# Scores of the first token tile as three float32r products in a two-layer decoder trunk

## The chip, the cores and the metric

The kernel runs on one core of a Trainium2 chip. The metric is the device time of one execution in microseconds (us), lower is better. Engines are called PE (TensorE, matrix products), DVE (VectorE), ACT (ScalarE), POOL (GpSimd) and SP (the DMA queue used for the weights).

## What is computed

Two decoder layers on 256 tokens of width 2048, in float32. The first layer normalises, projects to queries, keys, values and gates, and runs two attention mixers: A with 16 query heads on 2 key heads and a window of 128, B with 16 heads and a mixture of dilated windows. The second layer is a spatial gating unit and has no attention. What the change touches is the score of a query with the keys that it may see:

```python
nb = -(-L // BLK)
qb = _blocks(q, nb)
kb = _with_prev(_blocks(k, nb))
vb = _with_prev(_blocks(v, nb))
s = jnp.einsum('bgrnqd,bgnkd->bgrnqk', qb, kb) + bias[:, :, None]
s = jnp.where(_band_mask(nb, max_dist), s, NEG)
```

With blocks of 128 and 256 tokens there are two query tiles. The second sees the keys of both tiles (256), the first only its own (128).

## The kernel before, in words

**Split products.** A weight product in float32 is written as three products of float32r operands (`gemm`, L121 to L123): a high half times a high half, high times low and low times high. The high half is a cast by ACT (`whi`, L85), the low half the rest, taken by DVE (`wlo`, L86). A weight tile comes by SP's queue, is split once, four tiles ahead at most, and used in twelve products of 512 columns.

**Fillers.** Everything of attention is put between the weight products. `gemm` calls `fill()` after every second group of three products, which advances the first generator in the list `fillers` by one step. So the generators `attn_a` (twice) and `attn_b` (twice) yield after pieces of work: first transpositions of keys and queries, then `attention`. After this a scheduler settles the order on each engine from the program's order and its own estimate of times. So small shifts can appear in the order away from the lines that are edited.

**Queries and keys.** `pair_T` (L218) transposes two 128-column pieces of both token tiles into the one PSUM bank with the tag `t`: four PE instructions. `q_T` reads this bank three times: ACT writes the high half of the second tile's queries (L230), DVE the low half (L231), ACT a float32 copy of the first tile's queries, `q0` (L234). `k_T` reads it three times too: `kh` of both tiles by ACT (L246), `kl` by DVE (L247), and a float32 copy of the first tile's keys, `k0`, by ACT (L248). The next transpositions wait until the last of the three has read. In the trace the operands `q0`, `q1` are called `q`, and `k0` is `k`.

**Scores.** `scores` works on two heads, one on rows 0 to 63 of the arrays and one on rows 64 to 127, each into a bank of its own (tag `s`, two banks). The second tile's scores, 256 columns, are the three products of L298; the first tile's, 128 columns, one float32 product, L301. DVE then adds bias and mask and takes the maximum (L307, L311), ACT takes exponentials (L321, L323). `ptrans` transposes the probabilities through bank `t` (L331, copy `pt` L333), `pv` multiplies with the values (L345 to L347, 64 columns). There are four score blocks of two heads in each of four runs of `attention`, 16 in all.

Of the kernel before, what the change touches and what calls it, by code (L numbers as in the profile page):

```python
# [10 lines left out]
F32 = mybir.dt.float32  # L11
F32R = mybir.dt.float32r
# [5 lines left out]
P = 128  # L18
# [15 lines left out]
def trunk(ctx, tc, x, xT, ev_g, w_in0, w_kva, qk_g, sinks, w_out0, od_g, w_in1, v_g, w_sT, b_s,  # L34
# [10 lines left out]
    def c4(shape, name, dt=F32):  # L45
        return big.tile(shape, dt, tag="c4", name=name)
# [174 lines left out]

    def q_T(z, scale, box):

        q0 = c4([P, 4, P], nm("q0"))
        q1 = c4([P, 2, 4, P], nm("q1"), F32R)
        box.extend((q0, q1))
        for p0 in range(0, 4, 2):
            tp = pair_T(z, p0, 2)
            ps_ = slice(p0, p0 + 2)
            nc.scalar.activation(q1[:, 0, ps_, :], tp[:, :, P:2 * P], AF.Copy, scale=scale)  # L230
            nc.vector.scalar_tensor_tensor(q1[:, 1, ps_, :], tp[:, :, P:2 * P], scale,  # L231
                                           q1[:, 0, ps_, :].bitcast(F32),
                                           op0=ALU.mult, op1=ALU.subtract)
            nc.scalar.activation(q0[:, ps_, :], tp[:, :, 0:P], AF.Copy, scale=scale)  # L234
            yield

    def k_T(z, npair, box):

        k0 = c4([P, npair, P], nm("k0"))
        kh = c4([P, npair, S], nm("kh"), F32R)  # L240
        kl = c4([P, npair, S], nm("kl"), F32R)
        box.extend((k0, kh, kl))
        for p0 in range(0, npair, 2):
            tp = pair_T(z, p0, 2)
            ps_ = slice(p0, p0 + 2)
            nc.scalar.copy(kh[:, ps_, :], tp)  # L246
            nc.vector.tensor_tensor(kl[:, ps_, :], tp, kh[:, ps_, :].bitcast(F32), op=ALU.subtract)  # L247
            nc.scalar.copy(k0[:, ps_, :], tp[:, :, 0:P])  # L248
            yield

    def qk_norm(z):
# [22 lines left out]

    def attention(mix, h0, first_bias, qTb, kTb, vfn, ydst):

        (q0, q1), (k0, kh, kl) = qTb, kTb
        bts = [first_bias, None]
        st = {}
        grp = {}  # L280
# [1 line left out]
        def scores(i0):  # L282


            if i0 % 4 == 0:
                nmx = tiny.tile([P, 4, 2], F32, tag="nmx", name=nm("nmx"))
                mx = tiny.tile([P, 4, 2], F32, tag="mx", name=nm("mx"))
                l = tiny.tile([P, 4, 2], F32, tag="l", name=nm("l"))
                grp[i0 // 4] = (bts[i0 // 4], mx, nmx, l)
            bt, mx, nmx, l = grp[i0 // 4]  # L290
            pq = i0 // 2
            kp = (h0 + i0) // 8 if mix == 0 else pq
            sps = [psum("s", 2), psum("s", 2)]
            halves = [slice(0, 64), slice(64, 128)]
            for qpart, kpart, st_, en_ in ((0, kh, True, False), (0, kl, False, False),
                                           (1, kh, False, True)):
                for sp, half in zip(sps, halves):
                    nc.tensor.matmul(sp[:, 0:256], q1[half, qpart, pq, :], kpart[half, kp, :],  # L298
                                     start=st_, stop=en_)
            for sp, half in zip(sps, halves):  # L300
                nc.tensor.matmul(sp[:, 256:384], q0[half, pq, :], k0[half, kp, :],  # L301
                                 start=True, stop=True)
            for i, sp in zip((i0, i0 + 1), sps):
                h = h0 + i
                j = i % 4
                sb = m2([P, 384], nm("sb"))
                nc.vector.tensor_tensor_reduce(out=sb[:, 0:256], in0=sp[:, 0:256],  # L307
                                               in1=bt[:, j, :],
                                               scale=1.0, scalar=NEG, op0=ALU.add, op1=ALU.max,
                                               accum_out=mx[:, j, 1:2])  # L310
                nc.vector.tensor_tensor_reduce(out=sb[:, 256:384], in0=sp[:, 256:384],  # L311
                                               in1=bt[:, j, P:2 * P],
                                               scale=1.0, scalar=NEG, op0=ALU.add, op1=ALU.max,
                                               accum_out=mx[:, j, 0:1])
                if mix == 0:
                    nc.vector.tensor_scalar(nmx[:, j, :], mx[:, j, :], snk[:, h:h + 1], -1.0,
                                            op0=ALU.max, op1=ALU.mult)
                else:
                    nc.vector.tensor_scalar(nmx[:, j, :], mx[:, j, :], -1.0, None, op0=ALU.mult)  # L319
                pr = m2([P, 384], nm("pr"))  # L320
                nc.scalar.activation(pr[:, 0:256], sb[:, 0:256], AF.Exp, bias=nmx[:, j, 1:2],  # L321
                                     accum_out=l[:, j, 1:2])
                nc.scalar.activation(pr[:, 256:384], sb[:, 256:384], AF.Exp,  # L323
                                     bias=nmx[:, j, 0:1], accum_out=l[:, j, 0:1])
                st[i] = pr
# [371 lines left out]
```

## Time and profile before

| | |
|---|---|
| median of 3 runs | 1159.23 us (1159.16 to 1159.51) |
| the profiled execution | 1158.9 us, its span 1157.1 us |
| PE | busy 1149.3 us, 99% of the span, 5498 instructions |
| DVE | busy 641.3 us, 55% |
| ACT | busy 592.7 us, 51% |
| POOL | busy 115.5 us, 10% |
| granted clock of PE | 1.0 over the span |

The span runs from the first to the last instruction. A busy PE is not a PE at its peak: products overlap, so what one costs is read from the distance between starts, not from its duration. Attention's share of the span lies between about 91 us (first key transpositions) and 354 us (last transpositions of its result).

### The profile page before, as it was taken

How to read it: one execution, taken by the hardware profiler on the slowest of the kernel's cores; microseconds unless marked ns; L12 is line 12 of the kernel's file. 1: busy time of each engine (PE TensorE's matmuls, PEld its weight loads, DVE VectorE, ACT ScalarE, POOL GpSimd, SP SyncE). 2: the span in 40 equal slices, each digit the busy share in tenths (PEclk: the TensorE clock that was granted, in tenths of full speed). 3: DMA queues.
4: the chain of work that ended last, by engine and by line, in shares of the span. 5: the costliest groups of instructions: out<-in, count | busy, mean ns of one | idle time of the engine just before them, and what ended most of it. 6: DMA issues, size and time to landing. Idle time of an engine off the chain costs nothing.

```text
span 1157.1 us, 14468 instructions
## 1 busy us (share of the span) xinstructions
PE 1149.3 (99%) x5498; PEld 952.8 (82%) x5498; DVE 641.3 (55%) x823; ACT 592.7 (51%) x820; POOL 115.5 (10%) x69
## 2 busy tenths in 40 slices
PE   9999999999999999999999999999999999999998
PEld 7887787788788888888888888888888888888887
DVE  6586567556546565544546555555555555445443
ACT  6556664644654455445445445554554455333432
POOL 0132112113012000111110000000000000000000
PEclk9999999999999999999999999999999999999999
DMA  9676435546447555666666555555556555666661
GB/s 352 224 248 208 130 117 184 172 137 226 144 143 228 185 183 182 215 204 200 213 203 193 184 181 187 177 184 194 185 168 197 182 184 172 203 207 210 197 210 38
DMA packets 63638, 218.37 MB, mean 189 GB/s; under 512 B 7632, under 2 KB 10320, under 8 KB 63312
## 3 DMA queue, kind: packets, MB, share of 16 engines
q1 hardware_dynamic: 60352, 209.74, 56.2%
q0 software_dynamic: 2080, 7.34, 2.1%
q8 instruction: 43, 0.70, 0.2%
q10 hardware_dynamic: 1136, 0.36, 0.1%
q14 instruction: 27, 0.22, 0.1%
HBM read 215.32 MB, written 2.10 MB: 188 GB/s over the span
## 4 chain that ended last, share of the span: by engine, by line
PE 95%; DVE 1%; ACT 1%; DMA 1%; issue 1%; SPq 0%; ACTq 0%
PE g L121 30%; PE g L122 30%; PE g L123 30%; PE t L331 1%; DMA wraw<-in_w_in_dram 1%; ACT whi L85 1%; DVE wlo L86 1%; PE s L298 1%; PE u L347 1%; PE u L346 1%; PE t L385 1%; PE u L345 0%; PE t L218 0%; PE s L599 0%; PE s L600 0%
## 5 line engine op out<-in xcount | busy, mean ns | idle before, releaser
L86 DVE TENSOR_TENSOR wlo<-wraw,whi 128x1024 fp32r<-128x1024 f32 (+1 forms) x393 | 512.7, 1309 | 448.8 <-ACT whi L85 447.7
L85 ACT CAST whi<-wraw 128x1024 fp32r<-128x1024 f32 (+1 forms) x393 | 408.3, 1041 | 490.8 <-PE g L123 468.0
L121 PE MATMUL g<-whi,hTh 128*128 128x512 f32 (+1 forms) x1184 | 464.2, 392 | 0.0
L122 PE MATMUL g<-wlo,hTh 128*128 128x512 f32 (+1 forms) x1184 | 459.5, 388 | 0.6 <-DVE wlo L86 0.6
L123 PE MATMUL g<-whi,hTl 128*128 128x512 f32 (+1 forms) x1184 | 458.9, 388 | 0.0
L123 PEld LDWEIGHTS g<-whi,hTl 128*128 128x128 f32 x1184 | 222.6, 188 | 45.0
L121 PEld LDWEIGHTS g<-whi,hTh 128*128 128x128 f32 x1184 | 222.8, 188 | 44.6
L122 PEld LDWEIGHTS g<-wlo,hTh 128*128 128x128 f32 x1184 | 222.8, 188 | 44.0 <-DVE wlo L86 1.4
L121 PE MATMUL g<-whi,yTh 128*128 128x512 f32 (+1 forms) x416 | 156.2, 376 | 0.0
L122 PE MATMUL g<-wlo,yTh 128*128 128x512 f32 (+1 forms) x416 | 155.3, 373 | 0.0
L123 PE MATMUL g<-whi,yTl 128*128 128x512 f32 (+1 forms) x416 | 155.3, 373 | 0.0
L123 PEld LDWEIGHTS g<-whi,yTl 128*128 128x128 f32 x416 | 78.3, 188 | 14.1
L121 PEld LDWEIGHTS g<-whi,yTh 128*128 128x128 f32 x416 | 78.4, 188 | 13.6
L122 PEld LDWEIGHTS g<-wlo,yTh 128*128 128x128 f32 x416 | 78.4, 189 | 13.5
L608 POOL TENSOR_TENSOR y<-y,gt 128x1024 f32<-128x1024 f32 x8 | 19.2, 2404 | 344.9 <-ACT gt L191 344.9
L577 POOL TENSOR_TENSOR v<-v,gv 128x1024 f32<-128x1024 f32 x8 | 22.1, 2757 | 219.5 <-ACT junk L574 219.5
L191 ACT ACT_TABLE_LOAD x20 | 25.7, 1283 | 1.7 <-PE g L123 1.4
L272 POOL TENSOR_TENSOR bias<-bias,ba 128x1024 f32<-128x1024 f32 x8 | 21.9, 2738 | 31.1 <-DMA bias<-in_bias_dram 27.8
L321 ACT ACTIVATE pr<-sb,nmx 128x256 f32<-128x256 f32 x32 | 16.2, 506 | 9.9 <-DVE nmx L319 6.6
L333 ACT COPY pt<-t 128x384 f32<-128x384 f32 x32 | 15.0, 469 | 9.8 <-PE t L331 9.8
L307 DVE CUSTOM_DVE_ANT_0 sb<-s,bias 128x256 f32<-128x256 f32 x32 | 13.3, 414 | 9.1 <-PE s L301 8.1
L588 DVE SCALAR_TENSOR_TENSOR vl<-v,rstdv,vh 128x512 fp32r<-128x512 f32 x16 | 11.3, 749 | 12.4 <-ACT vh L587 12.4
(127 smaller groups left out, 555.2 us busy)
## 6 DMA issues: line engine op xcount, KB each, us to landing
wraw<-in_w_in_dram SPq DMA_DIRECT2D x287, 512.0 KB, 3.7
wraw<-in_w_out_dram SPq DMA_DIRECT2D x96, 512.0 KB, 4.0
bias<-in_bias_dram POOLq DMA_DIRECT2D x8, 512.0 KB, 3.8
xT<-in_xT_dram SPq DMA_DIRECT2D x8, 256.0 KB, 5.0
xr<-in_x_dram SPq DMA_DIRECT2D x2, 1024.0 KB, 11.1
wraw<-in_w_kva_dram SPq DMA_DIRECT2D x8, 256.0 KB, 3.4
gv<-in_v_g_dram POOLq DMA_DIRECT2D x8, 256.0 KB, 3.1
out_dram<-o SPq DMA_DIRECT2D x7, 256.0 KB, 5.1
```

What stands on the lines that cost most here:

```text
L85: nc.scalar.copy(hi[:, js, :cw], raw[:, js, :cw])
L86: nc.vector.tensor_tensor(lo[:, js, :cw], raw[:, js, :cw], hi[:, js, :cw].bitcast(F32), op=ALU.subtract)
L121: nc.tensor.matmul(o, ah[:, sl], whi[:, k, a:b], start=st, stop=False)
L122: nc.tensor.matmul(o, ah[:, sl], wlo[:, k, a:b], start=False, stop=False)
L123: nc.tensor.matmul(o, al[:, sl], whi[:, k, a:b], start=False, stop=en)
L191: nc.scalar.activation(z[:, tt, :cw], acc[tt][:, :cw], func, scale=rs[:, tt:tt + 1])
L272: nc.gpsimd.tensor_tensor(bt, bt, ba[:, mix:mix + 1, :].broadcast_to([P, 4, 256]), op=ALU.add)
L307: nc.vector.tensor_tensor_reduce(out=sb[:, 0:256], in0=sp[:, 0:256], in1=bt[:, j, :], scale=1.0, scalar=NEG, op0=ALU.add, op1=ALU.max, acc ...
L321: nc.scalar.activation(pr[:, 0:256], sb[:, 0:256], AF.Exp, bias=nmx[:, j, 1:2], accum_out=l[:, j, 1:2])
L333: nc.scalar.copy(pt, tp[:, 0:384])
L577: nc.gpsimd.tensor_tensor(v, v, gv.unsqueeze(1).broadcast_to([P, 2, 512]), op=ALU.mult)
L608: nc.gpsimd.tensor_tensor(y, y, gate[0], op=ALU.mult)
```

## The change

The queries of both tiles are now split into `qh` and `ql`, with one wide operation each on ACT and DVE, and the copies `q0` and `k0` and their two ACT operations are gone. The first tile's scores are three float32r products of 128 columns, like those of the second tile. In the list of buffers `c4` a run of `k_T` asks for two tiles and not three, `q_T` for two as before.

```diff
--- before.py
+++ after.py
@@ -221,31 +221,26 @@
 
     def q_T(z, scale, box):
 
-        q0 = c4([P, 4, P], nm("q0"))
-        q1 = c4([P, 2, 4, P], nm("q1"), F32R)
-        box.extend((q0, q1))
+        qh, ql = c4([P, 4, S], nm("qh"), F32R), c4([P, 4, S], nm("ql"), F32R)
+        box.extend((qh, ql))
         for p0 in range(0, 4, 2):
             tp = pair_T(z, p0, 2)
             ps_ = slice(p0, p0 + 2)
-            nc.scalar.activation(q1[:, 0, ps_, :], tp[:, :, P:2 * P], AF.Copy, scale=scale)
-            nc.vector.scalar_tensor_tensor(q1[:, 1, ps_, :], tp[:, :, P:2 * P], scale,
-                                           q1[:, 0, ps_, :].bitcast(F32),
+            nc.scalar.activation(qh[:, ps_, :], tp, AF.Copy, scale=scale)
+            nc.vector.scalar_tensor_tensor(ql[:, ps_, :], tp, scale, qh[:, ps_, :].bitcast(F32),
                                            op0=ALU.mult, op1=ALU.subtract)
-            nc.scalar.activation(q0[:, ps_, :], tp[:, :, 0:P], AF.Copy, scale=scale)
             yield
 
     def k_T(z, npair, box):
 
-        k0 = c4([P, npair, P], nm("k0"))
         kh = c4([P, npair, S], nm("kh"), F32R)
         kl = c4([P, npair, S], nm("kl"), F32R)
-        box.extend((k0, kh, kl))
+        box.extend((kh, kl))
         for p0 in range(0, npair, 2):
             tp = pair_T(z, p0, 2)
             ps_ = slice(p0, p0 + 2)
             nc.scalar.copy(kh[:, ps_, :], tp)
             nc.vector.tensor_tensor(kl[:, ps_, :], tp, kh[:, ps_, :].bitcast(F32), op=ALU.subtract)
-            nc.scalar.copy(k0[:, ps_, :], tp[:, :, 0:P])
             yield
 
     def qk_norm(z):
@@ -274,7 +269,7 @@
 
     def attention(mix, h0, first_bias, qTb, kTb, vfn, ydst):
 
-        (q0, q1), (k0, kh, kl) = qTb, kTb
+        (qh, ql), (kh, kl) = qTb, kTb
         bts = [first_bias, None]
         st = {}
         grp = {}
@@ -292,14 +287,12 @@
             kp = (h0 + i0) // 8 if mix == 0 else pq
             sps = [psum("s", 2), psum("s", 2)]
             halves = [slice(0, 64), slice(64, 128)]
-            for qpart, kpart, st_, en_ in ((0, kh, True, False), (0, kl, False, False),
-                                           (1, kh, False, True)):
-                for sp, half in zip(sps, halves):
-                    nc.tensor.matmul(sp[:, 0:256], q1[half, qpart, pq, :], kpart[half, kp, :],
-                                     start=st_, stop=en_)
-            for sp, half in zip(sps, halves):
-                nc.tensor.matmul(sp[:, 256:384], q0[half, pq, :], k0[half, kp, :],
-                                 start=True, stop=True)
+            for cs, qs, nk in ((slice(0, 256), slice(P, S), S), (slice(256, 384), slice(0, P), P)):
+                for q, k, st_, en_ in ((qh, kh, True, False), (qh, kl, False, False),
+                                       (ql, kh, False, True)):
+                    for sp, half in zip(sps, halves):
+                        nc.tensor.matmul(sp[:, cs], q[half, pq, qs], k[half, kp, 0:nk],
+                                         start=st_, stop=en_)
             for i, sp in zip((i0, i0 + 1), sps):
                 h = h0 + i
                 j = i % 4
```

In PE's order 64 products more appear (96 of 128 columns for 32). Three places of the order matter later. The first is ACT while mixer B's group 0 gets its keys and queries ready. Before:

```order
L246 CAST kh_1980<-t_1982 128x512
L85 CAST whi_2109<-wraw_2107 128x1024
L248 COPY k_1979<-t_1982 128x256
L246 CAST kh_1980<-t_1996 128x512
L85 CAST whi_2157<-wraw_2155 128x1024
L248 COPY k_1979<-t_1996 128x256
L230 ACTIVATE q_2017<-t_2018,gain 128x256
L234 ACTIVATE q_2016<-t_2018,gain 128x256
L85 CAST whi_2218<-wraw_2216 128x1024
L230 ACTIVATE q_2017<-t_2032,gain 128x256
L234 ACTIVATE q_2016<-t_2032,gain 128x256
```

After:

```order
L242 CAST kh_2005<-t_2007 128x512
L85 CAST whi_2134<-wraw_2132 128x1024
L242 CAST kh_2005<-t_2020 128x512
L85 CAST whi_2186<-wraw_2184 128x1024
L229 ACTIVATE qh_2039<-t_2041,gain 128x512
L85 CAST whi_2251<-wraw_2249 128x1024
L229 ACTIVATE qh_2039<-t_2054,gain 128x512
```

The copies `k` (that is `k0`) and the second `q` of each pair (`q0`) are gone; the casts `whi` of the weights move up between `kh` and `qh`. On PE the four groups of transpositions of this stage have 13, 12 and 7 weight products between them before, and 8, 10 and 12 after; in mixer A's group 1 the two groups of query transpositions have 13 before and 12 after.

The second place is DVE when mixer A's group 0 evacuates its first scores (`sb` and the maximum `mx`, one head after the other). Before:

```order
L231 SCALAR_TENSOR_TENSOR q_924<-t_945,gain,q_924 128x256
L307 ISA sb_991,mx_979<-s_981,bias_718 128x256
L307 ISA mx_979 128x1
L311 ISA sb_991,mx_979<-s_981,bias_718 128x128
L311 ISA mx_979 128x1
L86 TENSOR_TENSOR wlo_1167<-wraw_1164,whi_1166 128x1024
L316 TENSOR_SCALAR nmx_978<-mx_979,snk 128x2
L307 ISA sb_998,mx_979<-s_982,bias_718 128x256
```

After:

```order
L230 SCALAR_TENSOR_TENSOR ql_922<-t_942,gain,qh_921 128x512
L86 TENSOR_TENSOR wlo_1179<-wraw_1176,whi_1178 128x1024
L300 ISA sb_991,mx_975<-s_977,bias_718 128x256
L300 ISA mx_975 128x1
L304 ISA sb_991,mx_975<-s_977,bias_718 128x128
L304 ISA mx_975 128x1
L309 TENSOR_SCALAR nmx_974<-mx_975,snk 128x2
L300 ISA sb_998,mx_975<-s_978,bias_718 128x256
```

The low half `wlo` of a weight tile stood between the evacuations of the two heads and now stands ahead of both.

The third is PE in the last score block of mixer B's group 0, where the transpositions of probabilities of an earlier head (`t`) come between the products. `s_2228` and `s_2229` are the two heads' banks before:

```order
L298 MATMUL s_2228<-kl_1981,q_2017 128x256
L298 MATMUL s_2229<-kl_1981,q_2017 128x256
L298 MATMUL s_2228<-kh_1980,q_2017 128x256
L298 MATMUL s_2229<-kh_1980,q_2017 128x256
L331 MATMUL t_2206<-ident,pr_2133 128x128 x3
L301 MATMUL s_2228<-k_1979,q_2016 128x128
L301 MATMUL s_2229<-k_1979,q_2016 128x128
```

and `s_2261` and `s_2262` after:

```order
L294 MATMUL s_2261<-kl_2006,qh_2039 128x256
L294 MATMUL s_2262<-kl_2006,qh_2039 128x256
L294 MATMUL s_2261<-kh_2005,ql_2040 128x256
L324 MATMUL t_2239<-ident,pr_2162 128x128 x3
L294 MATMUL s_2262<-kh_2005,ql_2040 128x256
L294 MATMUL s_2261<-kh_2005,qh_2039 128x128
L294 MATMUL s_2262<-kh_2005,qh_2039 128x128
L294 MATMUL s_2261<-kl_2006,qh_2039 128x128
L294 MATMUL s_2262<-kl_2006,qh_2039 128x128
```

The transpositions fell between the wide and the narrow products; now they fall between the two heads' last wide products, and the narrow ones follow with the heads shifted by one. The last block of mixer B's group 1 changes alike. In the fourth block of mixer A's group 0 the two heads ran one after the other with one weight product between them (four products each); now one head's first five, the other's first five, and then the last product of each follow without a weight product between.

## Rows read from the trace of the kernel before

**Rows 1.** The page, part 4: the chain that ended last, by engine.
```profile
PE 95%; DVE 1%; ACT 1%; DMA 1%; issue 1%; SPq 0%; ACTq 0%
```

**Rows 2.** The waits of PE: engine, line, releaser, total us, times, longest.
```profile
PE t L218 <- ACT q L234: 1.2, 1, 1.2
...
PE g L122 <- DVE wlo L86: 0.6, 2, 0.4
...
PE t L218 <- ACT k L248: 0.2, 1, 0.2
PE t L331 <- ACT pt L333: 0.2, 1, 0.2
```

**Rows 3.** Timeline of PE, first score block: start us, us covered, instructions.
```profile
99.73 0.38 PE L298 MATMUL s<-kh,q 64*128 64x256 f32 x2
99.95 0.28 PE L298 MATMUL s<-kl,q 64*128 64x256 f32 x2
100.07 0.28 PE L298 MATMUL s<-kh,q 64*128 64x256 f32 x2
100.19 0.38 PE L301 MATMUL s<-k,q 64*128 64x128 f32 x4
100.50 0.50 PE L121 MATMUL g<-whi,hTh 128*128 128x512 f32 x1
```

**Rows 4.** Timeline of PE, products of probabilities and values in mixer A.
```profile
111.27 0.39 PE L346 MATMUL u<-kva,pt 128*128 128x64 f32 x2
111.49 0.39 PE L347 MATMUL u<-kva,pt 128*128 128x64 f32 x2
```

**Rows 5.** Timeline of PE, where weight products narrow from 512 to 256 columns.
```profile
50.77 0.39 PE L122 MATMUL g<-wlo,hTh 128*128 128x512 f32 x1
51.00 0.39 PE L123 MATMUL g<-whi,hTl 128*128 128x512 f32 x1
51.22 0.28 PE L121 MATMUL g<-whi,hTh 128*128 128x256 f32 x1
51.34 0.28 PE L122 MATMUL g<-wlo,hTh 128*128 128x256 f32 x1
```

**Rows 6.** Timeline of PE, fourth score block of mixer A, group 0: its ends.
```profile
113.25 0.38 PE L298 MATMUL s<-kh,q 64*128 64x256 f32 x1
...
115.22 0.50 PE L122 MATMUL g<-wlo,hTh 128*128 128x512 f32 x1
```

**Rows 7.** Timeline of all engines, before the second score block of group 0.
```profile
100.72 0.47 ACT L234 ACTIVATE q<-t,gain 128x256 f32<-128x256 f32 x1 [2.62 <-DVE q L231]
...
102.16 1.23 DVE L86 TENSOR_TENSOR wlo<-wraw,whi 128x1024 fp32r<-128x1024 f32 x1 [0.80 <-ACT whi L85]
...
103.44 0.38 PE L298 MATMUL s<-kh,q 64*128 64x256 f32 x1
...
104.13 0.38 PE L298 MATMUL s<-kh,q 64*128 64x256 f32 x1 [0.30 <-DVE mx L311]
```

**Rows 8.** Timeline of all engines, second query transpositions of mixer A, group 1.
```profile
136.47 0.47 DVE L231 SCALAR_TENSOR_TENSOR q<-t,gain,q 128x256 fp32r<-128x256 f32 x1
...
137.04 0.47 ACT L234 ACTIVATE q<-t,gain 128x256 f32<-128x256 f32 x1 [2.62 <-DVE q L231]
...
137.57 0.66 PE L218 MATMUL t<-ident,qa 128*128 128x128 f32 x4 [1.18 <-ACT q L234]
```

**Rows 9.** Timeline of all engines, third transpositions of mixer B, group 0.
```profile
211.04 0.69 DVE L247 TENSOR_TENSOR kl<-t,kh 128x512 fp32r<-128x512 f32 x1 [0.38 <-ACT kh L246]
...
212.74 0.39 PE L121 MATMUL g<-whi,hTh 128*128 128x512 f32 x1
212.86 0.36 ACT L248 COPY k<-t 128x256 f32<-128x256 f32 x1
...
213.37 0.63 PE L218 MATMUL t<-ident,zb 128*128 128x128 f32 x4 [0.24 <-ACT k L248]
```

**Rows 10.** The page, part 5: the same operation of DVE on 512 columns.
```profile
L588 DVE SCALAR_TENSOR_TENSOR vl<-v,rstdv,vh 128x512 fp32r<-128x512 f32 x16 | 11.3, 749 | 12.4 <-ACT vh L587 12.4
```

## The prediction

> **What bounds the kernel now.** I read the page's busy shares and its chain first, then the waits of TensorE (PE), then the stretches around the scores. PE is hardly ever idle (the table above) and carries 95% of the chain that ends last [rows 1]. So time is won or lost in two ways only: PE gets more or less to do, or it stands less or more in front of something late. PE waits for next to nothing: the list of its waits [rows 2] has 1.2 us for `q0` (the float32 copy of the first tile's queries), 0.2 us for `k0`, 0.2 us for `pt`, and 0.6 us for `wlo`, the low halves of the weights, in the whole run. VectorE (DVE) and ScalarE (ACT) work at about half load (the same table). The reader should keep that smallness in mind: whatever the change frees on ACT is worth nothing unless one of those waits hangs on it.
>
> The PE view of one score block [rows 3] shows the price of a product. The two heads of a pair sit on rows 0 to 63 and 64 to 127 and start together ("x2"), so I count passes of pairs. The three float32r passes of 256 columns follow each other by 0.22 (the first), 0.12 and 0.12 us. The float32 product of 128 columns is two passes: four records of about 0.27 us cover 0.38 us, so the second pass begins 0.11 us after the first. Then 0.20 us go by until the next weight product starts.
>
> **Part 1: the products.** Two float32 passes leave a block, three float32r passes of 128 columns come in. No float32r product under 256 columns is in the trace, so its pass is bounded. From below: products of 512 columns follow each other by 0.22 to 0.23 us and those of 256 by 0.12 us [rows 5], nearly in proportion, so 128 columns alone would take some 0.06 us. From above, in proportion to nothing: a 256-column pass takes 0.12 us [rows 3], and half the columns should not take more. In between stand the products of probabilities and values: their passes stream 64 columns and still follow by 0.11 us [rows 4]. The streaming is not what they wait for there, but the next 128x128 load of weights. The new passes load 128 columns of queries each, the same amount, so I take 0.11 us.
>
> The Trainium skill, page "TensorE: Matmul & The Clock Gate", section "Back-to-back issue gap", says that a stream of load and matmul pairs runs at about 81 ns per matmul of 128 columns at full clock. By that a block would change by 3 x 0.081 - 0.216, that is by some 0.03 us in place of the 0.11 below; the rows at 0.11 us with even fewer columns speak against it here.
>
> - 13 of the 16 blocks keep their form: three passes of 0.11 for two, +0.11 us each, **+1.4 us**.
> - The fourth block of mixer A, group 0, runs its two heads one after the other today, with a weight product between: from its first score to the next weight product but one are 1.97 us [rows 6], 1.74 without the 0.23 of that product. In the new order all twelve stand in one run, the second head begins beside the first one's last pass but one, and the last pass of both is shared. Ten steps of 0.22, 0.12, 0.12, 0.11, then 0.22, 0.12, 0.12, 0.11, 0.11 and the 0.20 at the end make 1.45: **-0.3 us**.
> - The last blocks of mixer B's groups are split today between passes by a group of transpositions. The new split falls half a pair earlier, so one head's `ql` pass runs with the other's first 128-column pass, and the rest stays shifted: two passes more than now, +0.23 us each, **+0.45 us**.
>
> Sum of part 1: +1.55 us on PE, where nothing covers it.
>
> **Part 2: the waits.** Every transposition of queries or keys goes through the only bank `t`, and the next group of four starts when the last reader has let go of it. Readers were three in a row; now there are two, the second longer.
>
> - Mixer A, group 1 [rows 8]. `wlo` holds DVE until 136.47, DVE's half then takes 0.47, ACT's `q0` starts at 137.04 and PE at 137.57. Now DVE's half has 512 columns, 0.75 us by the same operation at that size [rows 10], and PE could go at 136.47 + 0.75 + about 0.06 = 137.28. In the new order this group stands one weight product (0.23) earlier, so of the 0.29 only **-0.06 us** is gain. The wait stays, with another name.
> - Mixer B, group 0 [rows 9]. `kl` is done at 211.73, but the copy `k0` sits behind a `whi` on ACT until 213.2 and PE starts at 213.37, while 212.74 + 0.23 would have done: 0.40 us. Without `k0` the bank is free 1.5 us sooner, and though the order brings the groups closer (8, 10 and 12 weight products between them, not 13, 12 and 7) that suffices: **-0.40 us**. The shorter waits of this kind (the second query group there, and both in group 1) I put at **-0.4 us** together, an estimate by the rest of the `q0` and `k0` rows [rows 2] and as little as zero.
> - Mixer A, group 0 [rows 7]. `q0` holds ACT until 101.1, so `whi`, `wlo` (102.16) and then the evacuation of the first block's second head are late, and the second block's second head starts at 104.13, 0.69 after its first at 103.44. In the new order `wlo` goes ahead of both evacuations, and `whi` no longer waits for `q0`, only for its buffer. DVE's second half, done today when `q0` starts at 100.72, ends 0.28 later, near 101.0, `wlo` of 1.23 then near 102.2, and two evacuations, which I estimate at 0.7 each (from the end of that `wlo` at 103.4 to 104.1 there is one), end at 103.6 where they end at 104.1 now: **-0.3 us**, and it is tight.
> - `pt` [rows 2]: in the new order on ACT a `whi` stands behind it and not before it: **-0.2 us**.
>
> Sum of part 2: -1.35 us.
>
> **Costs put at nothing.** ACT loses eight `q0` copies of 0.47 [rows 8] and five `k0` copies of 0.36 [rows 9], 5.6 us, and gets eight wider `qh`. DVE's eight `ql` grow by 0.27 each, 2.2 us. Both lie beside PE as long as weights are split ahead of it; PE's 0.6 us for `wlo` in all [rows 2] is the evidence. If that cover went, 2.2 us would be the price. Three buffers of 27 fewer are asked for, and the orders of the DMA queue and of GpSimd are the same.
>
> **Sum.** +1.55 - 1.35 = +0.2 us on the profiled execution, 1158.9 to 1159.1. The median of the runs is 0.3 above that execution, so I forecast **1159.4 us**. Under 0.2%, 2.3 us either way, a measurement of this kernel can hardly tell from no change: 1156.9 to 1161.5 is "same".
>
> **Rivals.**
> 1. *Short float32r products are slow* (the one that ends slower). If 128 columns of float32r cost what a float32 product of 128 columns costs, 0.22 us for two passes [rows 3], then a block pays 3 x 0.22 - 0.22 = +0.43: 13 x 0.43 = 5.6, the unpaired block -0.3 + 5 x 0.11 = +0.25, the split ones 2 x 0.56 = 1.1, together +7.0, less the 1.35 of waits: 1164.8 us. For it: nothing under 256 columns is seen in this form. Against: 256 and 512 columns keep the one-column rate, and the same records appear for both. It decides at a pass of about 0.2 us. 13%.
> 2. *The passes stream without waiting for weights*, 0.06 us. Then a block pays 3 x 0.06 - 0.22 = -0.03, part 1 comes to about -0.6, and with the waits 1157.3 us. Against it: [rows 4]. The Trainium skill, page "TensorE: Matmul & The Clock Gate", section "Back-to-back issue gap", gives 56 ns as the gap of an isolated matmul of 128 columns at full clock, which would be this case. 12%.
> 3. *The waits don't go but change names.* The longer `ql` and the `wlo` placed ahead of the first evacuation keep PE as late as before: part 1 alone, 1160.8, and up to 1 us more where the second block waits for DVE longer than the 0.69 above: 1161.8. 15%.
> 4. *The wait in mixer A, group 1 goes too*, because a shifted GpSimd operation no longer slows that `wlo`; with rival 2 this is the only way to faster than 1156.9. 5%.
>
> **How the numbers follow.** My forecast has 55%. The range reaches from rival 2 to the worse end of rival 3, **1157.2 to 1162.0**, and leaves out rival 1 and a little on the other side. Faster 0.06 (rival 4, a bit of rival 2), slower 0.17 (rival 1, a quarter of rival 3), same 0.77.
>
> **What would show it.** In the changed profile the 128-column score passes should follow each other by 0.11 us; 0.06 or 0.22 would show rival 2 or 1. The waits for `q0` and `k0` should be gone from PE's list, with one of about 1.2 us for `ql` in their place; the gap at the third transposition group of mixer B, group 0, should be gone; the second block of mixer A, group 0, should start its heads less than 0.4 us apart. If all this holds and the time differs by over 2 us, the loss lies in `wlo` arriving late somewhere else, and the sum above was made over the wrong places.

## The result and the profile after

The changed kernel takes 1165.91 us in the median (1165.13 to 1167.62, 4 runs) where the kernel before takes 1159.29 beside it: 1.0060 times as long, 95% interval 1.0047 to 1.0072. The forecast was 1159.4 with a range to 1162.0. It is slower, by 6.6 us, and outside the range.

The profiled execution took 1166.41 us, its span is 1164.6. From its page (engines, granted clock by slices of 29 us, chain):

```profile
PE 1152.7 (99%) x5530; PEld 956.4 (82%) x5530; DVE 643.4 (55%) x823; ACT 589.9 (51%) x807; POOL 115.2 (10%) x69
...
PEclk9999989999999999999999999999999999999999
...
PE 94%; ACT 2%; DVE 2%; issue 1%; DMA 1%; SPq 0%; ACTq 0%
```

PE still carries the chain [rows 1], and DVE and ACT stay at half load. Two things are new: DVE and ACT have 2% each of the chain, and one slice, the sixth, which runs from 146 to 175 us, shows an 8 for the clock. The waits of PE (in all, times, longest):

```profile
PE s L294 <- DVE mx L304: 2.5, 3, 1.6
PE t L218 <- DVE kl L243: 1.3, 1, 1.3
PE g L121 <- ACT whi L85: 1.1, 1, 1.1
...
PE t L324 <- ACT pt L326: 0.9, 2, 0.5
...
PE g L122 <- DVE wlo L86: 0.5, 1, 0.5
PE t L218 <- DVE ql L230: 0.4, 1, 0.4
```

`q0` and `k0` are gone from the list [rows 2], as forecast. In their place stand `mx` (a score bank not yet evacuated), `kl` and more of `pt`. The `whi` row is not the change's: it stands at 10.16 us, with the first weight tiles, where the other profiles have 0 to 0.6 us. First, the products. PE in the first score block, the counterpart of [rows 3]:

```profile
100.40 0.38 PE L294 MATMUL s<-kh,qh 64*128 64x256 f32 x2
100.62 0.28 PE L294 MATMUL s<-kl,qh 64*128 64x256 f32 x2
100.74 0.28 PE L294 MATMUL s<-kh,ql 64*128 64x256 f32 x2
100.86 0.22 PE L294 MATMUL s<-kh,qh 64*128 64x128 f32 x2
100.92 0.27 PE L294 MATMUL s<-kl,qh 64*128 64x128 f32 x2
101.02 0.28 PE L294 MATMUL s<-kh,ql 64*128 64x128 f32 x2
...
101.23 0.50 PE L121 MATMUL g<-whi,hTh 128*128 128x512 f32 x1
```

The short passes follow each other by 0.06 and 0.10 us. From the first product to the next weight product the block takes 0.83 us, 0.77 before [rows 3]: +0.06 per block, about 1 us for 16 blocks. That is no 6.6 us.

Second, mixer A's group 1, where the slice with the lower clock lies. All engines, around the fourth block (start, us, instruction, idle before it):

```profile
151.54 0.20 ACT L349 ACTIVATE es<-es 128x8 f32<-128x8 f32 x1
...
151.72 1.89 POOL L198 TENSOR_TENSOR sq<-zb 128x1024 f32<-128x1024 f32 x1 [10.69 <-ACT zb L191]
151.77 1.86 DVE L350 TENSOR_TENSOR l<-l,es 128x8 f32<-128x8 f32 x1 [2.54 <-ACT es L349]
...
153.56 0.41 DVE L300 CUSTOM_DVE_ANT_0 sb<-s,bias 128x256 f32<-128x256 f32 x1
...
154.24 0.38 PE L294 MATMUL s<-kh,qh 64*128 64x256 f32 x1 [0.52 <-DVE mx L304]
...
154.36 1.21 DVE L200 TENSOR_REDUCE hs<-sq 128x16 f32<-128x1024 f32 x1
...
155.49 0.41 DVE L300 CUSTOM_DVE_ANT_0 sb<-s,bias 128x256 f32<-128x256 f32 x1
...
156.17 0.38 PE L294 MATMUL s<-kh,qh 64*128 64x256 f32 x1 [1.55 <-DVE mx L304]
```

The scores of the third block are finished, but DVE stands idle for 2.54 us: next in its queue is `l` (the sum of the softmax, L350), which needs `es` from ACT. `l`, 8 columns, then takes 1.86 us beside GpSimd's `sq`. Only then the first head's bank is evacuated (`sb`), then `hs` for a later norm takes 1.21 us, and only then the second head's. PE's fourth block needs both banks, and waits 0.52 and 1.55 us (the third wait for `mx`, 0.40 us, stands between the heads of the third block). What follows is read off the busy times by stretch (length, then busy us and instructions of PE, PEld, DVE, ACT, POOL, then the granted clock):

```profile
150.00:157.00 7.00, 4.92 (x32) 3.75 (x31) 5.23 (x14) 4.60 (x13) 1.89 (x1) 0.97 0.04 16
157.00:161.40 4.40, 4.02 (x15) 2.69 (x14) 4.12 (x18) 1.83 (x6) 0.59 (x1) 0.50 0.48 155
```

The granted clock is 0.50, the lower level of 1.2 GHz, for 4.4 us. Before it fell PE had been busy for 4.92 of 7 us. At half speed 4.4 us hold the work of 2.2. So 2.1 us of waits for `mx` there and 2.2 us of slow clock make over 4 us in one place.

Third, mixer B's group 1, at the third transpositions:

```profile
295.18 2.40 POOL L267 TENSOR_TENSOR bias<-bias,ba 128x1024 f32<-128x1024 f32 x1 [3.85 <-DMA bias<-in_bias_dram]
...
295.95 2.71 DVE L86 TENSOR_TENSOR wlo<-wraw,whi 128x1024 fp32r<-128x1024 f32 x1 [0.79 <-ACT whi L85]
298.58 0.68 DVE L243 TENSOR_TENSOR kl<-t,kh 128x512 fp32r<-128x512 f32 x1
...
299.41 0.63 PE L218 MATMUL t<-ident,zb 128*128 128x128 f32 x4 [1.25 <-DVE kl L243]
```

`wlo`, 1.22 us for the tile before, takes 2.71 beside GpSimd's addition to the bias tile, `kl` comes after it, and PE waits 1.25 us for bank `t`. The kernel before has a slowed `wlo` there too (2.22 us), but nobody waits behind it. The transpositions stand closer here than before (10 weight products after the second group, 12 before), since no `k0` reads the bank any more.

The Trainium skill, page "SBUF — State Buffer", section "Who interferes with whom", says that a DVE instruction with two SBUF inputs contends with a GpSimd instruction that reads SBUF. `l` and `wlo` are of that kind, and the rows agree: 1.86 us beside `sq`, and 0.15 for the same `l` in a run below where it came after `sq` had ended.

### The profile page after: what moved, and what is told of

The parts are those of the page before. It is cut to its first block, busy times and chain, and to the rows that moved or that the text cites. A ratio compares the mean times of both kernels' runs of the same rounds, so it can differ in the third digit from the quotient of the medians.

```text
span 1164.6 us, 14515 instructions
## 1 busy us (share of the span) xinstructions
PE 1152.7 (99%) x5530; PEld 956.4 (82%) x5530; DVE 643.4 (55%) x823; ACT 589.9 (51%) x807; POOL 115.2 (10%) x69
## 4 chain that ended last, share of the span: by engine, by line
PE 94%; ACT 2%; DVE 2%; issue 1%; DMA 1%; SPq 0%; ACTq 0%
PE g L121 30%; PE g L123 30%; PE g L122 30%; PE t L324 1%; DVE wlo L86 1%; ACT whi L85 1%; PE s L294 1%; PE u L340 1%; PE u L339 1%; PE t L378 1%; DMA wraw<-in_w_in_dram 1%; PE u L338 0%; PE t L218 0%; ACT pr L314 0%; ACT pr L316 0%
## 5 line engine op out<-in xcount | busy, mean ns | idle before, releaser
L324 PEld LDWEIGHTS t<-ident,pr 128*128 128x128 f32 x96 | 12.5, 145 | 6.4 <-ACT pt L326 2.7
```

Source lines behind the costliest of these rows:

```text
L324: nc.tensor.transpose(tp[:, b * P:(b + 1) * P], pr[:, b * P:(b + 1) * P], ident)
```

## The experiments

Three theories went into the first four runs. Theory 1: the order of DVE's queue in group 1 of mixer A, with the `kl` wait in B, is the loss. Theory 2: the short products cost it by themselves. Theory 3: the staging does, that is the missing copies and the wider halves. The changed kernel and all twelve runs:

| run | median us | ratio to the kernel before | 95% interval |
|---|---|---|---|
| the changed kernel | 1165.91 | 1.0060 | 1.0047 to 1.0072 |
| staging_only | 1159.01 | 0.9997 | 0.9986 to 1.0008 |
| products_only | 1165.22 | 1.0049 | 1.0031 to 1.0068 |
| order_l | 1164.30 | 1.0044 | 1.0030 to 1.0057 |
| order_l_hs | 1164.28 | 1.0048 | 1.0031 to 1.0064 |
| order_dve | 1163.03 | 1.0027 | 1.0017 to 1.0036 |
| order_dve_kl | 1161.66 | 1.0018 | 1.0006 to 1.0030 |
| one_narrow | 1158.30 | 0.9988 | 0.9979 to 0.9997 |
| before_order_after | 1160.41 | 1.0009 | 1.0000 to 1.0018 |
| order_all | 1161.46 | 1.0020 | 1.0010 to 1.0030 |
| order_all_T | 1159.36 | 1.0007 | 0.9998 to 1.0016 |
| staging_T | 1157.65 | 0.9986 | 0.9977 to 0.9995 |
| before_all_after | 1162.93 | 1.0034 | 1.0024 to 1.0043 |

The kernel before had a median of 1158.80 beside runs 2 to 5 of the table, 1159.47 beside the next four and 1159.08 beside the last four, so differences between batches are taken from the ratios (0.0010 is 1.16 us).

### One half of the change at a time

staging_only: the new `q_T` and `k_T`, but one float32 product of the high halves for the first tile; the low halves of that tile are left out of its scores.

```
-            for cs, qs, nk in ((slice(0, 256), slice(P, S), S), (slice(256, 384), slice(0, P), P)):
...
+            for sp, half in zip(sps, halves):
+                nc.tensor.matmul(sp[:, 256:384], qh[half, pq, 0:P].bitcast(F32),
+                                 kh[half, kp, 0:P].bitcast(F32), start=True, stop=True)
```

> The new splitting of queries and keys (no float32 copies, two readers of bank t), but the first tile's scores stay one float32 product of 128 columns, made of the high halves (their low halves are left out). Theory 1 (the loss is where DVE's order puts the add of the sink terms l and the reduction hs ahead of the evacuations in mixer A, group 1, plus the wait for kl in mixer B, group 1): DVE's order in group 1 of mixer A is here that of the kernel before, so the long waits at 148 to 157 us are gone and the wait for kl of about 1.3 us stays: 1159 to 1161 us. Theory 2 (the short float32r products themselves cost the time): the products are gone, so 1157.5 to 1159 us. Theory 3 (the missing copies and the wider splits cost it): 1164 to 1166 us.

products_only: the three short products, and the copies kept though nothing reads them.

```
+            nc.scalar.activation(q0[:, ps_, :], tp[:, :, 0:P], AF.Copy, scale=scale)
...
+            nc.scalar.copy(k0[:, ps_, :], tp[:, :, 0:P])
```

> The three float32r products, with the float32 copies of queries and keys still made by ACT (nobody reads them), so that bank t has three readers as before. Theory 1: DVE's order in mixer A, group 1, has l behind the third block's first evacuation but hs still between the two heads: a part of the waits, 1161 to 1165 us, and no wait for kl. Theory 2: 1165 to 1167 us with score blocks over 1.3 us long. Theory 3: 1159 to 1160 us.

In sum the staging changes nothing that can be measured (a gain and a loss that cancel, as staging_T shows below), the products bring 5.7 of the 7.0 us by the ratios, and theory 3 falls. The 1165.22 us of products_only lie in the range of theory 2 and 0.2 us above that of theory 1. But the waits in products_only have new names again, in the same place:

```profile
154.55 0.38 PE L298 MATMUL s<-kh,qh 64*128 64x256 f32 x1 [0.91 <-DVE mx L308]
156.28 0.65 PE L328 MATMUL t<-ident,pr 128*128 128x128 f32 x3 [1.10 <-ACT pt L330]
```

And staging_only has the order of the kernel before on DVE, instruction by instruction, and PE waits 0.2 us at most around the third and fourth block of mixer A's group 1. The rows that answer to those of the changed kernel:

```profile
148.72 0.42 DVE L302 CUSTOM_DVE_ANT_0 sb<-s,bias 128x256 f32<-128x256 f32 x1 [1.26 <-PE s L296]
...
149.69 1.86 DVE L352 TENSOR_TENSOR l<-l,es 128x8 f32<-128x8 f32 x1
...
151.71 0.37 DVE L302 CUSTOM_DVE_ANT_0 sb<-s,bias 128x256 f32<-128x256 f32 x1
...
152.22 1.22 DVE L200 TENSOR_REDUCE hs<-sq 128x16 f32<-128x1024 f32 x1
```

`l` is as slow here (1.86 us), but it is issued when `es` is ready and both evacuations are done by the time that `hs` begins. The price of `l` is the same; its place is not. Row by row, the orders of DVE in the kernel before and in the changed one differ between 101 and 168 us alone, that is in mixer A.

### Moving `l` and `hs` by hand

order_l puts `l` behind the evacuations of the block after it; order_l_hs puts `hs` behind them too.

```
+                    with behind(evac_done[min(i + 2, 7)]):
+                        nc.vector.tensor_tensor(l, l, es, op=ALU.add)
...
+        with behind(evac_done.get("last")):
+            nc.vector.tensor_reduce(s.rearrange("p (t h) -> p t h", t=2),
```

> The changed kernel with one thing more: on DVE the add of the sink terms l is queued behind the second head's evacuation of the score block that follows. The reduction hs then stands between the two heads of the third block in mixer A, group 1. Theory 1: the first wait of that block (0.5 us) goes, the second (1.6 us) stays or grows, because hs, ra and a wlo stand between the heads: 1163 to 1166 us. Theory 2: no difference from the changed kernel, 1165 to 1166 us.

> The changed kernel with l and the reduction hs both queued behind the evacuations of the two heads. Theory 1: the waits of 0.5 and 1.6 us in front of the fourth block and the slow clock that follows them go, some 5 us; the wait for kl of 1.3 us stays: 1159.5 to 1161.5 us. Theory 2: 1165 to 1166 us as before.

Both take 1164.3 us. For order_l this is in theory 1's range, and the rows show what it said: the first wait is gone, the second has grown. order_l_hs missed: theory 1 wanted 1159.5 to 1161.5 us, theory 2 at least 1165. Whatever is taken away, the scheduler puts something else there. In order_l the second head waits longest of all; in order_l_hs a `wlo` that has waited for its `whi` comes between the two heads, and `pt` is late after that. The first fence is order_l, the second order_l_hs:

```profile
155.81 0.38 PE L299 MATMUL s<-kh,qh 64*128 64x256 f32 x1 [2.48 <-DVE mx L309]
```

```profile
151.71 1.99 DVE L86 TENSOR_TENSOR wlo<-wraw,whi 128x1024 fp32r<-128x1024 f32 x1 [2.03 <-ACT whi L85]
...
153.62 0.41 DVE L306 CUSTOM_DVE_ANT_0 sb<-s,bias 128x256 f32<-128x256 f32 x1
...
154.31 0.38 PE L300 MATMUL s<-kh,qh 64*128 64x256 f32 x1 [1.27 <-DVE mx L310]
...
155.56 0.15 DVE L359 TENSOR_TENSOR l<-l,es 128x8 f32<-128x8 f32 x1
...
156.01 0.55 PE L332 MATMUL t<-ident,pr 128*128 128x128 f32 x3 [1.09 <-ACT pt L334]
```

So moving single instructions doesn't decide between theories 1 and 2; the whole queue has to be held.

### The whole order of DVE

order_dve takes the changed kernel and chains 110 instructions of DVE, numbered as traced, in the order of the kernel before. The chains are of issue order alone: they add no wait for another engine. before_order_after does the reverse to the kernel before, with the changed kernel's order in group 1 of A.

```
+def in_order(tc, queues):
+    for engine, numbers in queues.items():
+        own = [i for i in tc.nc.cur_bb.bb.instructions if str(i.engine) == "EngineType." + engine]
+        for a, b in zip(numbers, numbers[1:]):
+            tc.add_manual_dep(own[b], own[a].name,
...
+        in_order(tc, QUEUES)
```

> The changed kernel, with its three short products, in which VectorE's instructions of attention A stand in the order of the kernel before (110 of them chained one behind the other; PE's blocks and transpositions stay at the places of the changed kernel). Theory 1 (order: in the second group of A, l, hs or a wlo stands ahead of the third block's evacuations, PE waits 1.3 to 2.7 us there and then works some 4 to 6 us at half its clock): 1159.3 to 1161.5 us, the waits for mx below 0.5 us in all, no stretch at 1.2 GHz in the third block of that group; what is left over the kernel before is about 1 us for the products (0.06 us in each of 16 blocks) and up to 2 us for the wait for kl in the second group of B. Theory 2 (the short products cost it by themselves, wherever they stand): 1163.5 us or more, with the gaps in other places.

> The kernel before, with its float32 product and its copies, in which VectorE's instructions of the second group of A alone stand in the order of the changed kernel. Theory 1 (order): PE waits 1 to 2.5 us for mx or pt at the third block of that group, then works at half clock, and the time is 1162 to 1166 us. Theory 2 (the short products): 1158.8 to 1160.3 us, since no product is changed.

Neither run came out in a range of theory 1 or theory 2. order_dve wins back about 3.8 us of 7 by the ratios (1.0060 to 1.0027), but not all; before_order_after loses 1.0 us, under the 3 to 7 that theory 1 wanted. The rows of order_dve show where the rest is: the waits for `mx` are gone, and PE stands in the middle of the fourth block.

```profile
152.59 1.22 DVE L200 TENSOR_REDUCE hs<-sq 128x16 f32<-128x1024 f32 x1
...
153.72 0.22 DVE L309 TENSOR_SCALAR nmx<-mx,snk 128x2 f32<-128x2 f32 x1
...
154.03 0.51 ACT L314 ACTIVATE pr<-sb,nmx 128x256 f32<-128x256 f32 x1 [2.18 <-DVE ra L63]
...
154.93 0.45 ACT L326 COPY pt<-t 128x384 f32<-128x384 f32 x1
...
155.43 0.55 PE L324 MATMUL t<-ident,pr 128*128 128x128 f32 x3 [1.82 <-ACT pt L326]
...
155.91 0.33 PE L294 MATMUL s<-kl,qh 64*128 64x128 f32 x2
```

The transpositions `t` of an older head's probabilities now stand on PE between the first and the second short product of the fourth block. They need bank `t`, which ACT's `pt` frees, and that is queued behind `pr`, which waits for `nmx` behind `hs`. In the kernel before and in staging_only six weight products stand between this block's end and those transpositions, in the changed kernel two. So PE's order differs as well, and I had held DVE's alone; with DVE held, the scheduler settled PE's anew, and the run is not the changed kernel with only DVE's order put back, as its expectation has it. A second wait for `pt`, 1.50 us at 116.60 in group 0, and 0.50 us for `kl` in B are left too.

before_order_after is not pure either: the transpositions behind its fourth block stand nine weight products off, where the kernel before has six. Its profile has no wait for `mx`. What it has and the kernel before has not is 0.87 us for `pt` at 165.22, 1.05 us for `k0` in B's group 1, where PE's order is that of the kernel before and a `wlo` takes 3.09 us beside GpSimd, and a wait at 98 us of which the last section tells.

one_narrow (order_dve with one float32r product for the first tile; its two correcting products are left out) came back with the block whole:

```
+                nc.tensor.matmul(sp[:, 256:384], qh[half, pq, 0:P], kh[half, kp, 0:P],
+                                 start=True, stop=True)
```

> As the kernel with VectorE's old order, but the first tile's scores are one float32r product of the high halves (the two correcting products of the first tile are left out): 64 products of 128 columns fewer. If PE bounds the kernel and a short product costs what the rows of the changed kernel show (0.057 or 0.11 us apart, 0.08 in the mean), it takes about 5 us less than the kernel with all three: 1154 to 1156.5 us where that one takes 1159.3 to 1161.5. If a short product costs 0.11 us throughout: 7 us less. If PE's time is not what bounds the blocks: less than 2 us.

It takes 4.5 us less than order_dve (ratios 0.9988 and 1.0027), near the 5 expected (the range, 1154 to 1156.5, was missed), but for a partly wrong reason. I had counted 64 products of 0.08 us, though the two heads of a pair run together in 32 passes. From its first product to the next weight product a whole block takes 0.61 us here and 0.83 in the changed kernel: 0.22 us per block, 3.5 us for 16. The rest I put down to PE's order, which is not the same in the two. Against order_all below, which has its order, one_narrow is 3.7 us faster.

order_dve_kl also puts the second `kl` of B's group 1 ahead of that slow `wlo`.

```
+    "DVE": [311, 312, 324],
```

> As the kernel with VectorE's old order; besides, in the second group of B the second kl stands ahead of the wlo that was before it on VectorE (PE's order there is held as it was). If that wlo, slowed to 2.7 us beside GpSimd's addition to the bias tile, is what made the third transpositions wait: their wait of 1.3 us for kl goes, and the time is 1 to 1.9 us below the other kernel's if that one shows the wait, the same where it does not. If the wait then stands at the wlo's product: no gain.

The wait for `kl` is gone from its list, and the ratio is lower by 0.0009, 1.0 us, but the intervals overlap. Its profiled execution, 1165.72 us, is one of the two slowest of its eleven. By itself this run settles nothing.

### Both engines' order, and the transpositions of B

By now theory 3 of the first runs had fallen. In the expectations of the last four runs "theory 3" is a new one: the order of both engines, PE's and DVE's, in group 1 of A, which the scheduler changes because the blocks are longer. order_all holds PE too: its instructions stand as in staging_only, each block's six short products where that kernel has its two. It chains 285 instructions of DVE, where order_dve has 110, and 1257 of PE.

```
+    "PE": [
...
+        in_order(tc, QUEUES)
```

> The changed kernel with its three short products, in which PE's instructions too (gemm products 400 to 1200) stand as in the kernel with the new staging and one float32 product, each block's six short passes where that one has its two; VectorE's order as there. Theory 3 (it is the order of both engines in the second group of A: longer blocks make the scheduler put transpositions of older heads ahead of or inside the fourth block's neighbourhood, where they wait for pt from ScalarE, and l, hs, wlo ahead of evacuations): 1159.5 to 1161 us, that is the 1159.0 of that kernel and 16 blocks by 0.06 us; no wait for mx or pt above 0.6 us, no stretch at 1.2 GHz. Theory 1 alone (VectorE's order is all): the same as the kernel with VectorE's order only, 1163.0. Theory 2 (the short products cost it wherever they stand): 1162.5 us or more.

order_all_T holds the second to fourth transpositions of B's group 1 where the kernel before has them, staging_T does this to staging_only (so the first tile's low halves are left out there as well). order_all_T differs from order_all by numbers in that list alone; staging_T is staging_only with both engines chained in its own order, but for these transpositions.

> As the kernel with both orders; besides, in the second group of B the second to fourth transpositions stand where the kernel before has them, after 1075, 1087 and 1094 products instead of 1070, 1080 and 1092, so that the second kl is read out before the third transpositions come. If the wait for kl there (1.3 us in the changed kernel, 1.9 us with one float32 product) is lost time: 1 to 2 us less than the kernel with both orders, 1158 to 1159.5 us. If something downstream takes the time back: no gain.

> The new staging with one float32 product of the high halves for the first tile, both engines' orders held, and the transpositions of the second group of B where the kernel before has them. If the wait of 1.9 us for kl is all that keeps the new staging from its gain: 1157 to 1158.3 us, under the kernel before by 1 to 2 us. If not: 1159.0 as without it.

before_all_after is the kernel before, with its float32 product and copies, under the changed kernel's order of PE and DVE in group 1 of A.

> The kernel before, its float32 product and copies kept, with the order of the changed kernel in the second group of A on both engines (VectorE as in the run with VectorE's order alone; PE's blocks, transpositions and PV products between its gemm products 552 and 640 as the changed kernel has them). Theory 3: PE waits 1 to 2.5 us about the third and fourth block and works some us at half clock, 1162.5 to 1165.5 us. Theory 2 (short products): 1159 to 1160.8 us, no more than VectorE's order alone gave.

order_all missed its range by half a us, at 1161.46, and is 4.6 us better than the changed kernel by the ratios, with intervals well apart. Waits of PE in its profile:

```profile
PE t L324 <- ACT pt L326: 0.9, 1, 0.9
PE t L218 <- DVE kl L243: 0.9, 1, 0.9
```

No wait for `mx` is left, and its profile shows no lower clock. The one for `pt` (0.9 us, at 161.54) is more than the 0.6 that I had allowed.

before_all_after shows the other side: the old products under the new order cost 3.9 us (1.0024 to 1.0043), as theory 3 said and theory 2 did not. Not all of it lies in the stretch whose order was changed. In group 1 of A PE's waits have moved to `pt` and come to 3.0 us (0.2 in the kernel before); 1.05 us is a wait for `k0` in B, where PE has the order of the kernel before. The half clock that theory 3 named too is not there: the granted clock of its profile is 1.00 in that stretch. The second fence, its timeline, shows one of the waits for `pt`, behind the same block as in the changed kernel, and the one for `k0`:

```profile
PE t L331 <- ACT pt L333: 2.7, 2, 1.4
```

```profile
156.05 0.55 PE L331 MATMUL t<-ident,pr 128*128 128x128 f32 x3 [1.29 <-ACT pt L333]
...
294.22 0.66 PE L218 MATMUL t<-ident,zb 128*128 128x128 f32 x4 [1.05 <-ACT k L248]
```

The transpositions of B give 1.5 us in order_all_T and 1.3 in staging_T. Each interval alone overlaps its neighbour's, but the two agree, and so do the waits: 0.9 us for `kl` in order_all and none in order_all_T, 1.92 in staging_only and none in staging_T. First staging_only's row, then staging_T's waits:

```profile
290.16 0.65 PE L218 MATMUL t<-ident,zb 128*128 128x128 f32 x4 [1.92 <-DVE kl L243]
```

```profile
PE t L218 <- DVE ql L230: 1.1, 1, 1.1
...
PE g L122 <- DVE wlo L86: 1.1, 2, 0.5
...
PE t L326 <- ACT pt L328: 0.2, 1, 0.2
```

How long this wait is, the order does not settle alone. With the same order of PE in B's group 1 it is 1.25 us in the changed kernel, 0.70 in order_l_hs, 0.50 in order_dve and none in order_l, where GpSimd's addition began 0.60 us after the `wlo` (1.23 us) and not before it. The addition starts when its bias tile has landed (the row at 295.18 above waits for that DMA), and that time shifts from profile to profile.

staging_T is the fastest kernel of the study, 1157.65 us, 1.6 us under the kernel before (0.6 to 2.7), but at the price of the left-out halves. No run chained a kernel in exactly its own order; that the chains themselves cost little is inferred from this one, which is chained throughout. The best one that computes all products is order_all_T at 1159.36: no different from the kernel before.

So the loss of 7.0 us (by the ratio) is made up, in steps between neighbouring runs:

| step | from, to | us |
|---|---|---|
| wider staging, fewer readers of bank `t` | before, staging_T | -1.6 |
| three short products in place of one, at the same order | staging_T, order_all_T | +2.4 |
| transpositions of B's group 1 closer together | order_all_T, order_all | +1.5 |
| PE's and DVE's order, mostly in A's group 1 | order_all, changed | +4.6 |

Each step is uncertain by 1 us or more. Of the 2.4 us for the products, rows show 1.0 as passes and 0.7 as a longer wait for `pt` (0.9 us, 0.2 in staging_T).

## Why the prediction was wrong

**The bound was right.** PE carries the chain before and after, and time was lost by work on PE and by waits in front of it.

**The products (part 1) were put too high, by 1.2 us.** I took 0.11 us for a short pass; the rows show 0.06 and 0.10, +0.06 per block in place of +0.11. The split blocks cost 0.1 us each (1.62 and 1.68 us, 1.54 before) and not 0.23. The fourth block of A's group 0 gained 0.7 us and not 0.3: from its first product to the next weight product it takes 1.06 us, 1.74 before without the weight product between its heads.

```profile
113.29 0.38 PE L294 MATMUL s<-kh,qh 64*128 64x256 f32 x1
...
114.35 0.50 PE L121 MATMUL g<-whi,hTh 128*128 128x512 f32 x1
```

By the rows part 1 comes to about +0.3 us in place of +1.55, so this error does not explain the loss; without it the forecast would have been lower still. Rival 1, slow short products, gave 1164.8 us, close to what was measured, but by luck, for its mechanism is refuted: no pass in these rows takes 0.2 us. The 81 ns of the Trainium skill, page "TensorE: Matmul & The Clock Gate", section "Back-to-back issue gap", would have made +0.03 per block; the +0.06 of the rows lies between that and my 0.11.

**The waits named in part 2 mostly went.** `q0` and `k0` left the list, and the second block of A's group 0 has its heads together. The wait for `ql` in A's group 1 was 0.4 us in the changed kernel, where I expected 1.2. The wait for `pt`, which I let go (-0.2 us), grew to 0.9.

**One step of part 2 failed in sign.** "The shorter waits of this kind", both in group 1 of B included, were put at -0.4 us and "as little as zero". There the new order brought the transpositions closer, on the argument that fewer readers suffice, and a `wlo` slowed by GpSimd to 2.71 us stood ahead of `kl`: a wait of 1.25 us in the profile, and 1.5 us of time in the run that undid it. My check of that argument was made at group 0 alone, where it holds (at 217.64 PE does not wait).

**The step that failed most is one that is not in the sum.** "13 of the 16 blocks keep their form" priced the passes of the blocks and took the neighbours of a block as they were. I compared the orders at three places close to the edited lines; A's group 1 has its block whole in both kernels, and I gave it -0.06 us for its transpositions. But there `l`, `hs` and a `wlo` on DVE, and the transpositions of probabilities on PE, had changed places. The runs put 4.6 us on this order, and 3.9 us with the old products, 1 us of which stands in B. Rival 3 had the kind of thing (a DVE instruction ahead of an evacuation) and the wrong block and size: up to 1 us in group 0, where the trace shows a gain.

**The clock was not in the sum at all.** A wait of 2 us was priced at 2 us. In the changed kernel's profile the half clock behind it cost as much again. My last sentence, that a loss of over 2 us would lie in a late `wlo` and the sum be made over the wrong places, is right on the places; a `wlo` it was in B, ahead of `kl`, but in A the instructions were mainly `l` and `hs`.

## What to carry to other kernels

Where a scheduler sets the order, a change of 0.06 us in a block can move instructions far from it, and what they wait for can cost many times the block's own change. So go through every place where the order of an engine differs, not those near the edit, and ask of each moved instruction what it waits for when it is issued and which evacuation now stands behind it. To learn whether a loss comes from an edit or from the order that came with it, hold the order and run both ways: the new work in the old order, and the old work in the new.

## What was not expected

- Behind waits of about 2 us PE sometimes works at half clock and sometimes not. order_dve's profile has 1.82 us of waiting at 155.43 and stays at clock 1.0 afterwards; order_dve_kl has 1.84 us at the same place of the same order, and its granted clock is 0.54 in the mean from 160.6 to 164.0 us. The changed kernel is at 0.50 for 4.4 us. The times of order_dve spread from 1159.8 to 1165.0 us: three runs with a granted clock of 1.000 over their span took 1159.8 to 1162.1, the eight with 0.998 or 0.999 took 1162.0 to 1165.0. What decides between the two was not tested.
- A DVE addition of 8 columns takes 1.86 us beside a GpSimd operation of 1.89, and 0.15 us alone. `wlo` grows from 1.22 to 2.71.
- Where the two engines meet is not fixed by the order. The profiles of order_dve_kl and before_order_after wait 2.08 and 1.91 us for the first group's queries at 98 us, as no other profile does: a `wlo` there starts at the same time as GpSimd's bias addition, to 0.3 us, and takes 3.45 and 3.26 us. In order_dve, which has the same order in A, that addition starts after the `wlo` has ended (1.23 us). How much of the spread of the times comes from this was not tested.
- Short float32r passes do not all cost the same: the second follows the first by 0.06, the third the second by 0.10.
